# Second sweep of a hybrid encoder layer: key and rotary-query transposes on VectorE in 32x32 blocks, blocks put in place by the loads

## The chip, the cores and the metric

The kernel runs on one core of one Trainium2 chip. The metric is the device time in microseconds of one execution; the shown time of the kernel before is the median of three runs, 1270.41 us (1268.89 to 1271.71). All engines of the core run side by side and wait for each other through semaphores: TensorE (PE in the profile, PEld for its weight loads), VectorE (DVE), ScalarE (ACT), GpSimd (POOL), and SyncE (SP), which here does nothing but issue DMA transfers. A transfer that an engine issues runs on 16 shared DMA engines.

## The reference

One encoder layer over 2048 tokens of width 1024. The input projection feeds two groups of heads, their gated outputs are concatenated and projected, and a residual with layer norm closes the layer. Cut to what the change touches:

```python
h = x @ w_in      # split: g_q g_k g_v g_gate g_lr_f g_lr_b | m_cq m_ckv m_kr m_gate
# group A: gated linear attention, forward and backward scans, 4 heads of 128
o = rms_norm(o_fwd + o_bwd, norm_g)
o_a = o * silu(gate)
# group B: latent attention, 4 heads
q = (rms_norm(c_q, q_norm_g) @ w_uq)            # per head: 128 plain, 64 rotary
kv = (rms_norm(c_kv, kv_norm_g) @ w_ukv)        # per head: 128 key, 128 value
k_r = apply_rope(k_rope, positions)             # one rotary key of 64 for all heads
s = einsum(q_nope, k_nope) + einsum(apply_rope(q_rope), k_r)
o_b = (softmax(s) @ v) * silu(gate)
out = layer_norm(ALPHA * x + concat(o_a, o_b) @ w_out)
```

The kernel takes the key projection into the queries (absorbed weights), so the scores are products of a 128-wide query with the 128-wide normed latent `ckv` itself, and the values are `ckv` too, projected afterwards. Every product is done in three matmuls of a high and a low part (`hi`, `lo`), which is how single precision is kept.

## The kernel before

Tokens are split in 16 chunks of 128. Four parts follow each other.

**Sweep A** goes backward over the chunks and computes most of group A; intermediate tensors go to DRAM.

**Sweep C** (the second sweep, `sweep_c`, about 347 to 583 us) goes forward in eight steps of two chunks. For each chunk it projects `cq`, `ckv` and the rotary key (`c_ip`, PE), norms them, and has PE transpose four 128x128 pieces by a matmul with the identity (`c_tm`, L1368): two of `cq`, one of `ckv`, and one of `krs`, which holds the high and the low part of the rotary key side by side. ACT and DVE then split the results into high and low parts in SBUF (`c_cqTh`, `c_cqTl`, `c_ckvTh`, `c_ckvTl`, `c_krT`). These, `ckvT_h`, `ckvT_l` and `kr`, stay in SBUF for attention, beside the untransposed `vh` and `vl`, which are the high and low parts of `ckv` and serve as values. From `cqT` come the plain queries of a step (`c_pq`) and the rotary queries of a chunk (`c_pqr`); the latter go through the rotation on DVE and POOL (`c_qrf`, `c_qrfa`), two transposes on PE (`c_tq`, L1408), a split (`c_qrTh`, `c_qrTl`), and to DRAM (`c_sqr`, four transfers a step). `c_Ob` to `c_og` finish group A's output of a chunk; `c_oT` transposes it on DVE, which turns every 32x32 block on its own and leaves the blocks where they were, and `c_soT` puts the blocks in place as it stores, in four transfers of 32 partitions whose contiguous pieces are 128 bytes long.

**Attention** runs 16 blocks of one head and 512 queries. `fetch` loads a block's queries: `qh`, `ql`, `rh`, `rl`. The rotary ones have 64 rows, and each is loaded twice, into both halves of the partitions, since `kr` has the high part of the key in one half and the low part in the other. `scores` runs five matmuls per key tile: two with `ckvT_h`, one with `ckvT_l`, two with `kr` (L1562 to L1566).

**The output product** (`OutProj`) loads a chunk's gated outputs of both groups (`load`: `of`, `gr`), multiplies group B's by its gates, splits both in high and low, multiplies with `w_out`, and closes with residual and layer norm.

The order of the work within an engine's queue in sweep C is written by hand: each operation has a place in a table (`PLACE_C`, with other values for the first and the last step), in units of a step, one value for each of the step's two chunks (the tuple) or one for the step. All operations are sorted by step number plus place, and every engine, SP too, runs its own in that order. An instruction that waits holds up whatever stands behind it on its engine. In a step, `tm` of its first chunk stands at 0.532 and of its second at 1.152, which is in the next step's time. The PSUM pool `tr` has two buffers, shared by `tm`, `pqr` and `tq`.

Of the kernel before, what the change touches and what calls it, by code (L numbers as in the profile page):

```python
# [9 lines left out]
F32 = mybir.dt.float32  # L10
F32R = mybir.dt.float32r
# [123 lines left out]
STEP_C = ("gm1", "gm2", "gm3", "gm4", "sgm", "pq", "qah", "qal", "sqa", "sqr")  # L135
CHUNK_C = ("lx", "xh", "xl", "lS", "lq", "lo", "lu", "sqm", "ssm", "rml", "rmd", "cq", "ckv", "krf", "krfa",
    "krsh", "krsl", "vh", "vl", "tm", "cqTh", "cqTl", "ckvTh", "ckvTl", "krT", "pqr", "qrf", "qrfa",
# [3 lines left out]
FETCH_C = ("lx", "xh", "xl")  # L141


PLACE_C = dict(
    ipa=(-0.08, 0.695),
# [6 lines left out]
    tq=(1.06, 1.482),  # L152
# [12 lines left out]
    qrTh=(1.16, 1.587),  # L165
# [11 lines left out]
    qrTl=(1.25, 1.687),  # L177
# [24 lines left out]
    sqr=1.869,  # L202
# [15 lines left out]
PLACE_C_FIRST = dict(  # L218
    ipa=(-1.874, 0.381),
# [6 lines left out]
    tq=(1.11, 1.512),  # L226
# [49 lines left out]
    sqr=1.92,  # L276
# [9 lines left out]
    tq=(0.919, 2.161),  # L286
# [49 lines left out]
    sqr=3.147,  # L336
# [10 lines left out]
class K:  # L347
# [146 lines left out]
    def run(self):  # L494
        tc, nc, ins = self.tc, self.nc, self.ins
        with ExitStack() as top:
# [43 lines left out]
            self.ckvT_h = rp.tile([P, NKT, P], F32R, name="ckvT_h")  # L540
            self.ckvT_l = rp.tile([P, NKT, P], F32R, name="ckvT_l")
            self.kr = rp.tile([P, NKT, P], F32R, name="krs")
# [586 lines left out]

    def split_c(self, xf, j, eng="pool"):  # L1130
        self.hi(self.xch[:, :, j], xf)
        self.lo(self.xcl[:, :, j], xf, self.xch[:, :, j], eng)

    def sweep_c(self):


        with ExitStack() as ctx:
# [17 lines left out]
            for s in steps:  # L1155
                for n in range(8):
                    put("pz", s["st"], self.c_pz, s, n, j=n)
                for n in STEP_C:
                    put(n, s["st"], getattr(self, "c_" + n), s)
            for d in chunks:  # L1160
                for n in range(4):
                    put("ip" + "abcd"[n], d["st"], self.c_ip, d, n, j=d["j"])
                for n in CHUNK_C:
                    if (d["st"] or n not in FETCH_C) and (d["c"] < NCH - 1 or n not in ("Sf1", "Sf2")):
                        put(n, d["st"], getattr(self, "c_" + n), d, j=d["j"])
            for i, place in enumerate((8.23, 9.35)):
# [44 lines left out]
    def scale_w(self, ct):  # L1211
        wa = self.w1.tile([P, H, P], F32, tag=f"qrT{'hl'[ct]}", name=f"wabs{ct}")
# [75 lines left out]
    def c_sqr(self, s):  # L1288
        b, qs = self.of_step(s)
        for t, dst in zip(s["qrT"], self.qr_s[b]):  # L1290
            for pr in range(2):
                self.nc.sync.dma_start(dst[2 * pr:2 * pr + 2, :, qs].rearrange("h d t -> (h d) t"),
# [767 lines left out]
```

## Time and profile before

| | |
|---|---|
| median of the runs shown | 1270.41 us |
| the profiled execution, its own time | 1270.53 us |
| its span (first to last instruction) | 1268.4 us |
| PE busy | 1247.2 us |
| DVE / ACT / POOL busy | 893.5 / 727.9 / 718.6 us |
| DMA engines, share of the span (queue q1) | 43.2% |
| transposes of sweep C on PE: tm, tq | 64, 32 instructions |
| block transposes of oT on DVE | 16, 712 ns each |
| packets under 512 bytes in sweep C (360 to 580 us) | 33629 |

The span is a little shorter than the time of the run, which has 2.1 us around it. In the views of the profile a row names the source line and engine, then what is written and read (`tm<-ident,ckv`). In rows of a timeline the first number is when the instruction starts, the second how long it takes, and brackets hold the idle time of the engine just before it and what ended that. The busy time of PE counts matmuls from their start to a modelled end, and they overlap: one matmul's length is more than the time by which it moves the next. A row of SP is the issue of a transfer; that it has landed is seen in the column "us to landing" of the DMA view or in who waits for it. The chain that ended last follows the work back from the last instruction, each time to what released it.

### The profile page before, as it was taken

How to read it: one execution, taken by the hardware profiler on the slowest of the kernel's cores; microseconds unless marked ns; L12 is line 12 of the kernel's file. 1: busy time of each engine (PE TensorE's matmuls, PEld its weight loads, DVE VectorE, ACT ScalarE, POOL GpSimd, SP SyncE). 2: the span in 40 equal slices, each digit the busy share in tenths (PEclk: the TensorE clock that was granted, in tenths of full speed). 3: DMA queues.
4: the chain of work that ended last, by engine and by line, in shares of the span. 5: the costliest groups of instructions: out<-in, count | busy, mean ns of one | idle time of the engine just before them, and what ended most of it. 6: DMA issues, size and time to landing. Idle time of an engine off the chain costs nothing.

```text
span 1268.4 us, 19649 instructions
## 1 busy us (share of the span) xinstructions
PE 1247.2 (98%) x6950; PEld 1100.2 (87%) x6950; DVE 893.5 (70%) x1610; ACT 727.9 (57%) x1177; POOL 718.6 (57%) x443
## 2 busy tenths in 40 slices
PE   8999999999999999989999999999999999999997
PEld 7999999999899999988788888888888888887886
DVE  6635555553665545564888888888888888389997
ACT  7544343454665444444888888888888888411110
POOL 0132323223265554430798888889999999935541
PEclk9999999999999999999999999999999999999999
DMA  8224555565857766747211111202133120376662
GB/s 297 76 82 124 136 144 137 144 134 159 274 173 211 210 187 204 211 133 199 76 32 53 40 45 42 59 9 59 58 92 92 42 42 26 122 231 195 208 191 100
DMA packets 188546, 160.10 MB, mean 126 GB/s; under 512 B 97206, under 2 KB 139838, under 8 KB 188448
## 3 DMA queue, kind: packets, MB, share of 16 engines
q1 hardware_dynamic: 180384, 156.72, 43.2%
q0 software_dynamic: 672, 2.10, 0.4%
q8 instruction: 55, 0.90, 0.3%
q10 hardware_dynamic: 7392, 0.03, 0.3%
q14 instruction: 43, 0.35, 0.1%
HBM read 102.79 MB, written 56.00 MB: 125 GB/s over the span
## 4 chain that ended last, share of the span: by engine, by line
PE 87%; issue 3%; DMA 3%; POOL 2%; DVE 2%; ACT 2%; SPq 1%; DVEq 0%; POOLq 0%; ACTq 0%
PE pz L1244 7%; PE ipm L1315 5%; PE o L412 5%; PE o L413 5%; PE o L414 4%; PE pS L1562 4%; PE pS L1563 4%; PE pS L1564 4%; PE pS L1565 4%; PE pS L1566 4%; PE ipa L412 4%; PE ipa L414 4%; PE ipa L413 4%; PE ipg L414 2%; PE ipg L413 2%
## 5 line engine op out<-in xcount | busy, mean ns | idle before, releaser
L364 POOL TENSOR_TENSOR pl<-s,ph 128x1024 fp32r<-128x1024 f32 x128 | 306.7, 2415 | 51.5 <-ACT ph L358 48.0
L1584 DVE TENSOR_TENSOR rm<-pS,rm 128x512 f32<-128x512 f32 x210 | 144.8, 690 | 36.3 <-ACT s L1571 30.7
L1571 ACT ACTIVATE s<-pS 128x1024 f32<-128x1024 f32 x128 | 131.2, 1025 | 61.3 <-PE pS L1566 51.7
L1608 DVE TENSOR_TENSOR s<-s,mb 128x1024 f32<-128x1024 f32 x128 | 151.2, 1213 | 8.9 <-PE mb L1602 8.2
L358 ACT ACTIVATE ph<-s 128x1024 fp32r<-128x1024 f32 x128 | 135.0, 1056 | 17.2 <-PE o L414 16.5
L1612 ACT ACTIVATE s<-s 128x1024 f32<-128x1024 f32 x128 | 131.4, 1049 | 9.4 <-DVE s L1608 9.3
L412 PE MATMUL ipa<-wah,xah 128*128 128x384 f32 (+1 forms) x384 | 128.8, 335 | 5.5 <-ACT wah L358 5.5
L413 PE MATMUL ipa<-wal,xah 128*128 128x384 f32 (+1 forms) x384 | 124.5, 324 | 0.0
L414 PE MATMUL ipa<-wah,xal 128*128 128x384 f32 (+1 forms) x384 | 124.5, 324 | 0.0
L1079 POOL TENSOR_TENSOR Sb<-Sb,Us 64x512 f32<-64x512 f32 x15 | 19.9, 1324 | 169.7 <-DVE Us L1071 160.6
L1562 PE MATMUL pS<-qh,ckvT_h 128*128 128x512 f32 x256 | 102.6, 401 | 0.8 <-DVE rm L1584 0.4
L412 PE MATMUL o<-ph,vh 128*128 128x512 f32 x256 | 101.1, 395 | 0.0
L1563 PE MATMUL pS<-ql,ckvT_h 128*128 128x512 f32 x256 | 100.0, 391 | 0.0
L1564 PE MATMUL pS<-qh,ckvT_l 128*128 128x512 f32 x256 | 99.9, 390 | 0.0
L1565 PE MATMUL pS<-rh,krs 128*128 128x512 f32 x256 | 99.9, 390 | 0.0
L1566 PE MATMUL pS<-rl,krs 128*128 128x512 f32 x256 | 99.8, 390 | 0.0
L414 PE MATMUL o<-ph,vl 128*128 128x512 f32 x256 | 99.8, 390 | 0.0
L413 PE MATMUL o<-pl,vh 128*128 128x512 f32 x256 | 99.7, 389 | 0.0
L1635 DVE TENSOR_TENSOR ap<-ap,s 128x512 f32<-128x512 f32 x120 | 83.0, 692 | 2.7 <-ACT s L1612 0.7
L412 PEld LDWEIGHTS ipa<-wah,xah 128*128 128x128 f32 x384 | 73.1, 190 | 8.4 <-ACT wah L358 5.5
L364 POOL TENSOR_TENSOR ol<-of,oh 128x512 fp32r<-128x512 f32 x32 | 43.0, 1344 | 64.3 <-ACT oh L358 64.3
L413 PEld LDWEIGHTS ipa<-wal,xah 128*128 128x128 f32 x384 | 73.2, 191 | 0.8 <-DVE wal L364 0.2
(302 smaller groups left out, 3427.3 us busy)
## 6 DMA issues: line engine op xcount, KB each, us to landing
xcf<-xT_dram SPq DMA_DIRECT2D x16, 512.0 KB, 5.4
xr<-x_dram SPq DMA_DIRECT2D x16, 512.0 KB, 6.3
out_dram<-rr SPq DMA_DIRECT2D x32, 256.0 KB, 2.1
xaf<-xT_dram SPq DMA_DIRECT2D x14, 512.0 KB, 4.2
oib<-oi_s SPq DMA_DIRECT2D x16, 256.0 KB, 3.7
qdb<-qd_s SPq DMA_DIRECT2D x16, 256.0 KB, 3.5
SU<-su_s SPq DMA_DIRECT2D x16, 256.0 KB, 3.9
ub<-u_s SPq DMA_DIRECT2D x16, 256.0 KB, 3.9
```

Of the source, the lines that this page charges most:

```text
L358: return nc.scalar.activation(dst, src, AF.Copy).ins
L364: return e.tensor_tensor(dst, src, hi.bitcast(F32), ALU.subtract).ins
L412: mm(out, ah, bh, start=start, stop=False)
L413: mm(out, ah, bl, start=False, stop=False)
L414: mm(out, al, bh, start=False, stop=stop)
L1562: mm(ps[:, e], kh, qh, start=True, stop=False)
L1563: mm(ps[:, e], kh, ql, start=False, stop=False)
L1564: mm(ps[:, e], kl, qh, start=False, stop=False)
L1565: mm(ps[:, e], kr, rh, start=False, stop=False)
L1566: mm(ps[:, e], kr, rl, start=False, stop=True)
L1584: V.tensor_tensor(d["rm"], src[:, e], d["rm"], ALU.max)
L1608: V.tensor_tensor(s, s, d["mb"][:, None, :].to_broadcast([P, 2, QB]), ALU.subtract)
```

## The change

Four things in sweep C and what reads from it.

**Keys.** For the chunks of the first seven steps `tm` transposes `cq` alone. A new operation `kvx` has DVE turn `vh`, `vl` and `krs` in 32x32 blocks into one tile per step; `skv` stores the tile as it lies, one transfer a step; `kv_load` brings two chunks back, one step and a bit later, in four transfers of 32 partitions, each block at its place. The splits `ckvTh`, `ckvTl` and `krT` go for these chunks: the high and the low part are turned, not split again. The last step's two chunks keep the old way. The three key tensors are now views of one tile, `kvT`.

**Rotary queries.** `tq` is DVE's: one 128x256 block transpose into SBUF. The splits read that tile, both parts go into one tile `qrT` (two buffers), and `sqr` is one transfer a chunk. `fetch` places the blocks: eight transfers a block of attention for `rh` and `rl`, where there were four.

**Gated output of group A.** `soT` stores `oT` as it lies in one transfer; `OutProj.load` places the blocks with four transfers of 32 partitions, where there was one.

**Places.** `tq`, `qrTh`, `qrTl` move back by up to 0.08; in the last step the loads `lq` and `lo`, `soT` and `tq` get other places, `lq` so that the first chunk's comes before the second's. `krs` has two buffers.

```diff
-STEP_C = ("gm1", "gm2", "gm3", "gm4", "sgm", "pq", "qah", "qal", "sqa", "sqr")
+STEP_C = ("gm1", "gm2", "gm3", "gm4", "sgm", "pq", "qah", "qal", "sqa")
...
+LAST_C = ("ckvTh", "ckvTl", "krT")
+KV_LOADS = tuple((2 * s - 4, 2 * s - 2, float(s)) for s in range(2, NCH // 2)) + ((12, 14, 8.27),)
...
 PLACE_C = dict(
+    skv=1.6,
+    kvx=(1.12, 1.44),
...
-    tq=(1.06, 1.482),
+    tq=(1.13, 1.56),
...
-    qrTh=(1.16, 1.587),
+    qrTh=(1.19, 1.62),
...
-    qrTl=(1.25, 1.687),
+    qrTl=(1.26, 1.7),
...
-    sqr=1.869,
+    sqr=(1.4, 1.88),
...
 PLACE_C_LAST = dict(
...
-    tq=(0.919, 2.161),
+    tq=(0.95, 2.1),
...
-    lq=(-0.287, -0.357),
-    lo=(-0.124, 0.045),
+    lq=(-0.357, 0.05),
+    lo=(-0.14, 0.045),
...
-    soT=(1.09, 2.304),
+    soT=(1.29, 2.304),
...
-    sqr=3.147,
+    sqr=(1.6, 3.147),
...
-            self.qr_s = [[dp.tile([H, 64, QB], F32, name=f"r{p}_s{b}") for p in "hl"] for b in range(NQB)]
+            self.qr_s = [dp.tile([2, QB // P, P, 256], F32, name=f"qr_s{b}") for b in range(NQB)]
...
-            self.oa_s = [dp.tile([P, H, P], F32, name=f"oa_s{c}") for c in range(NCH)]
+            self.kv_s = dp.tile([NCH, 3, P, P], F32, name="kv_s")
+            self.oa_s = [dp.tile([H, P, P], F32, name=f"oa_s{c}") for c in range(NCH)]
...
+    def blocks_of(self, src):
+
+        v = src.rearrange("i (b r) m t -> m r (i b) t", b=4)
+        return [(slice(32 * m, 32 * m + 32), v[m]) for m in range(4)]
...
+    def c_kvx(self, d):
+
+        s = d["step"]
+        if "kvx" not in s:
+            s["kvx"] = self.w1.tile([P, 2, 3, P], F32, tag="kvx", name=f"kvx{d['st']}")
+        for i, src in enumerate((self.vh[:, d["c"]], self.vl[:, d["c"]], d["krs"].rearrange("p a d -> p (a d)"))):
+            self.nc.vector.transpose(s["kvx"][:, d["j"], i], src.bitcast(F32))
+
+    def c_skv(self, s):
+        c = 2 * s["st"]
+        self.nc.sync.dma_start(self.kv_s[c:c + 2].rearrange("c i p f -> p (c i) f"),
+                               s["kvx"].rearrange("p a i f -> p (a i) f"))
+
+    def kv_load(self, cs):
+        for r, src in self.blocks_of(self.kv_s[cs].rearrange("c i p (m t) -> (c i) p m t", t=32)):
+            self.nc.sync.dma_start(self.kvT[r, cs].rearrange("p c i (b t) -> p (c i b) t", t=32).bitcast(F32), src)
...
-        for i, src in enumerate((d["cq"][:, 0:P], d["cq"][:, P:2 * P], d["ckv"],
-                                 d["krs"].rearrange("p a d -> p (a d)").bitcast(F32))):
-            self.nc.tensor.transpose(tp[:, i], src, self.ident)
+        src = (d["cq"][:, 0:P], d["cq"][:, P:2 * P])
+        if d["st"] == NCH // 2 - 1:
+            src += d["ckv"], d["krs"].rearrange("p a d -> p (a d)").bitcast(F32)
+        for i, e in enumerate(src):
+            self.nc.tensor.transpose(tp[:, i], e, self.ident)
...
     def c_tq(self, d):
-        tq = d["tq"] = self.tr.tile([P, 4, P], F32, tag="tr", name=f"tq{d['c']}")
-        for pr in range(2):
-            self.nc.tensor.transpose(tq[:, pr], d["qr"][:, 2 * pr:2 * pr + 2].rearrange("p h d -> p (h d)"), self.ident)
+        d["tq"] = self.w1.tile([P, 256], F32, tag="qrx", name=f"qrx{d['c']}")
+        self.nc.vector.transpose(d["tq"], d["qr"].rearrange("p h d -> p (h d)"))
...
     def c_soT(self, d):
-        t = d["oT"].rearrange("p h (a t) -> p h a t", a=4)
-        dst = self.oa_s[d["c"]].rearrange("(a r) h (b t) -> b r h a t", a=4, b=4)
-        for b in range(4):
-            self.nc.sync.dma_start(dst[b], t[32 * b:32 * b + 32])
+        self.nc.sync.dma_start(self.oa_s[d["c"]].rearrange("h p f -> p h f"), d["oT"])
...
-        for p, src in zip("hl", self.qr_s[b]):
+        for n, p in enumerate("hl"):
             q.append(qp.tile([P, QB], F32R, tag="wz", name=f"r{p}{i}"))
-            for r in (slice(0, 64), slice(64, 128)):
-                nc.sync.dma_start(q[-1][r].bitcast(F32), src[h])
+            src = self.qr_s[b][n].rearrange("c (b r) (m t) -> m r (c b) t", b=4, t=32)
+            for r in range(4):
+                nc.sync.dma_start(q[-1][32 * r:32 * r + 32].rearrange("p (c t) -> p c t", t=32).bitcast(F32),
+                                  src[2 * h + r % 2])
...
-        nc.sync.dma_start(of[:, 0], kern.oa_s[c])
+        for r, src in kern.blocks_of(kern.oa_s[c].rearrange("h p (m t) -> h p m t", t=32)):
+            nc.sync.dma_start(of[r, 0].rearrange("p h (b t) -> p (h b) t", t=32), src)
```

More of the change, by code (lines that the diff above doesn't have):

```diff
@@ L218 @@
 PLACE_C_FIRST = dict(
+    skv=1.6,
+    kvx=(1.18, 1.5),
     ipa=(-1.874, 0.381),
@@ L1163, in sweep_c @@
                 for n in CHUNK_C:
+                    late = d["st"] == len(steps) - 1
+                    if n in (LAST_C if not late else ("kvx",)):
+                        continue
                     if (d["st"] or n not in FETCH_C) and (d["c"] < NCH - 1 or n not in ("Sf1", "Sf2")):
                         put(n, d["st"], getattr(self, "c_" + n), d, j=d["j"])
+            for a, b, place in KV_LOADS:
+                todo.append((place, len(todo), self.kv_load, (slice(a, b),)))
             for i, place in enumerate((8.23, 9.35)):
@@ L1351, in c_krsh @@
     def c_krsh(self, d):
-        d["krs"] = self.w1.tile([P, 2, 64], F32R, tag="krs", name=f"krs{d['c']}")
+        d["krs"] = self.w1.tile([P, 2, 64], F32R, tag="krs", name=f"krs{d['c']}", bufs=2)
         self.hi(d["krs"][:, 0], d["kr"][:, 0])
```

33 lines of the change are left out of this document (18 added, 15 removed).

## The prediction

> **What bounds the kernel now.** I read the page first: busy shares, the slices, the chain that ended last. Then, for the second sweep, the windows by step, the waits of PE, the chain of one step in order of time, and the timelines of SP, DVE and PE at the two places where a transfer could come late.
>
> ```profile
> span 1268.4 us, 19649 instructions
> PE 1247.2 (98%) x6950; PEld 1100.2 (87%) x6950; DVE 893.5 (70%) x1610; ACT 727.9 (57%) x1177; POOL 718.6 (57%) x443
> PE 87%; issue 3%; DMA 3%; POOL 2%; DVE 2%; ACT 2%; SPq 1%; DVEq 0%; POOLq 0%; ACTq 0%
> ```
>
> PE is busy 98% of the span and is 87% of the chain. That share alone would not say that a PE instruction taken out shortens anything, so the windows come next (us, then busy time of PE, PEld, DVE, ACT, POOL, then clock, DMA share, GB/s): one middle step of the second sweep, 218 us of that sweep, a stretch of attention, and six chunks of the output product.
>
> ```profile
> 435.36:463.90 28.54, 28.54 (x210) 27.80 (x210) 15.48 (x57) 14.10 (x41) 14.97 (x17) 1.00 0.71 204
> 362.00:580.00 218.00, 214.78 (x1553) 207.90 (x1552) 119.11 (x431) 105.55 (x304) 105.32 (x115) 0.99 0.66 189
> 640.00:1000.00 360.00, 360.00 (x1654) 298.05 (x1653) 312.94 (x419) 301.31 (x324) 317.54 (x136) 1.00 0.20 52
> 1183.74:1249.02 65.28, 65.28 (x290) 54.08 (x289) 63.55 (x89) 8.85 (x23) 31.42 (x24) 1.00 0.57 184
> ```
>
> A middle step lasts 28.54 us and PE has no idle time in it, while DVE works 15.48 and ACT 14.10. So a step is as long as its matmuls take to issue, and the whole sweep lacks only 3.22 us of PE work (218.00 - 214.78). Attention and the output product are as full: what the sweep saves isn't eaten by a later stage that waits for something fixed.
>
> **Transposes removed.** The chain in order of time through 460 to 468 us has what a transpose costs:
>
> ```profile
> 463.68 0.22 PE tq L1408 x2
> 463.90 0.89 PE Ob L1462 x8
> 464.79 0.44 PE tm L1368 x4
> 465.23 2.88 PE pz L1244 x24
> L1368 PE MATMUL tm<-ident,ckv x16: 272/273/273, 363.2 to 576.0; 128*128 128x128 f32 x16
> L1408 PE MATMUL tq<-ident,qrf x32: 270/272/328, 377.9 to 582.7; 128*128 128x128 f32 x32
> ```
>
> Two of tq move the chain by 0.22 us and four of tm by 0.44: 0.11 us each, though the tile views give 272 ns as the length of one. PE is pipelined; the step pays the interval, not the length. The change takes out both tq transposes of 16 chunks (32), and the ckv and krs transposes of 14 chunks, since the last step keeps its own (28). 60 x 0.11 = **6.6 us** off PE. Nothing is added to PE. The Trainium skill (TensorE: Matmul & The Clock Gate, Part 4) gives about 275 ns for a 128x128 transpose inside a kernel; by that 60 would be worth 16.5 us. The trace agrees with it as a length, not as what the next matmul waits.
>
> **VectorE.** Added per chunk: three 128x128 block transposes (kvx) and one 128x256 (tq). Removed: the low part of ckvT. The shapes next to them:
>
> ```profile
> L1014 DVE STREAM_TRANSPOSE ktx<-kd 128x512 f32<-128x512 f32 x10 | 6.7, 674 | 0.0
> ...
> L817 DVE STREAM_TRANSPOSE qx<-ipa 128x256 f32<-128x256 f32 x12 | 5.3, 441 | 0.0
> L1491 DVE STREAM_TRANSPOSE oT<-og 128x512 f32<-128x512 f32 x16 | 11.4, 712 | 0.5
> 467.35 0.42 DVE L364 TENSOR_TENSOR cqT_l<-tm,cqT_h 128x256 fp32r<-128x256 f32 x1
> 469.62 0.28 PE L414 MATMUL pqr<-wqr_h,cqT_l 128*128 128x256 f32 x1
> ```
>
> From 441 and 674 ns, 256 columns cost 0.23 us, so 128 columns take 0.32 and a chunk adds 3 x 0.32 + 0.44 = 1.40 us. By the places in the tables, all four stand in front of cqTl of the step's second chunk, and PE waits for cqTl: it ends at 467.77 and L414, the first matmul that reads cqT_l, issues at 469.62. That is 1.85 us of room, less 0.44 because four transposes ahead of it on PE are gone: 1.41. So the addition just fits and costs **0**; without that cover it is on the path in every step. Upper bound: all four at 0.712, 2.85 us, 1.44 late in 7 steps, 10.1 us. A gain is excluded, since PE has no idle time there to give back. At the first chunk of a step kvx and tq stand where DVE idles before qal. ACT loses two copies a chunk and gains nothing.
>
> **DMA engines and SP.** Key store (skv), key load (kv_load), plain oT store and rotary-query store replace four oT stores a chunk and four rotary stores a step. Packets of 128 bytes exist before as stores only; a window with nothing else in it, then the tail's queue:
>
> ```profile
> DMA packets 544, 0.07 MB, mean 51 GB/s; under 512 B 544, under 2 KB 544, under 8 KB 544
> q1 hardware_dynamic: 544, 0.07, 34.2%
> ...
> q1 hardware_dynamic: 33995, 36.11, 42.8%
> L1497 SPq DMA_DIRECT2D oa_s<-oT x64: 580/632/1392, 375.9 to 587.0; - x64
> L1897 SPq DMA_DIRECT2D of<-oa_s x16: 325/384/791, 940.7 to 1221.1; - x16
> ```
>
> The first window is 1.3 us: 0.342 x 16 x 1.3 us / 544 = 13 ns a packet. The tail (268 us) gives 54 ns for a mean packet of 1062 bytes; on the line between, 512 bytes cost 30 ns. A step's DMA work is 0.71 x 28.54 = 20.3 us. Off: 4096 packets of 13 ns over 16 engines, 3.3. On: 1792 rows of 512 bytes, 3.4, and 3072 loaded pieces of 128 bytes. No load of such pieces can be read here by itself. Bounds 13 ns (same size, stored) and 54 ns (mean load of the tail); I take 13, as the size is the same: 2.5 us, 22.9 of a 27.65 us step. It fits, cost **0**. The step is full at 38 ns. SP loses 8 x 0.63 (oT) and gains about 0.4 x 2 and 4 x 0.63 to 0.95 (kv_load): no more than before. What newly waits on SP is the key store, for kvx of the second chunk; behind it stands the qdb load of the next chunk, whose product comes over half a step later.
>
> **The step before the last.** PE's waits in the sweep, and what led to them:
>
> ```profile
> PE pqr L412 <- DVE rm_t L431: 2.6, 1, 2.6
> ...
> PE pqr L414 <- DVE cqT_l L364: 0.3, 1, 0.3
> PE tq L1408 <- POOL qrf L1403: 0.2, 1, 0.2
> 535.26 9.54 SPq L1423 DMA_DIRECT2D qdb<-qd_s  x2
> 544.89 0.74 SPq L1423 DMA_DIRECT2D SU<-su_s  x1
> 545.72 0.86 SPq L1292 DMA_DIRECT2D rh_s<-qrTh  x2
> 546.67 0.90 SPq L1292 DMA_DIRECT2D rl_s<-qrTl  x2
> 547.62 0.94 SPq L1423 DMA_DIRECT2D oib<-oi_s  x2
> 547.93 1.05 PE L1462 MATMUL Ob<-SU,qdb 128*128 128x128 f32 x8
> 551.40 0.70 DVE L1465 TENSOR_TENSOR Ob<-Ob,oib 128x512 f32<-128x512 f32 x1 [3.51 <-DMA oib<-oi_s]
> ```
>
> That is all of the 3.2 us: SP issues the oib load only at 547.62, behind four rotary stores; DVE stands until 551.40, and cqTl is late. The changed order puts oib of chunk 14 ahead of the last rotary store, about 2.4 us earlier, so DVE could start when Ob is done (548.98). It then has 1.40 us more to do before cqTl, so the stall ends 1.0 earlier, of which 0.44 are transposes already counted: **-0.6**, bounds 0 and -3.2.
>
> **Start of attention.** Loads of the first block's queries, and the matmul that needs the last of them:
>
> ```profile
> 575.03 0.62 SPq L1532 DMA_DIRECT2D qh<-qh_s  x1
> 577.45 1.19 SPq L1536 DMA_DIRECT2D rl<-rl_s  x2
> 583.69 0.39 PE L1566 MATMUL pS<-rl,krs 128*128 128x512 f32 x1
> rl<-rl_s SPq DMA_DIRECT2D x32, 128.0 KB, 4.6
> ```
>
> Issue ends at 578.64 and the data land by about 582.7, 1 us ahead of use. Rotary queries now need eight issues of 0.63 instead of four of 0.6: 2.6 us more. But the oT store that ran just ahead of them (4 x 0.63 us) is now behind, so **0**, bounds 0 and +1.6 (2.6 less the 1 us).
>
> **Output product.** The load of a chunk's gated part is four issues, 2.2 us more SP time ahead of the ob_s load. It is near the path once:
>
> ```profile
> 1115.04 0.53 SPq L1900 DMA_DIRECT2D of<-ob_s  x1
> 1126.02 2.55 POOL L364 TENSOR_TENSOR ol<-of,oh 128x512 fp32r<-128x512 f32 x2 [0.74 <-ACT oh L358]
> 1126.19 0.39 PE L412 MATMUL pmb<-woh,oh 128*128 128x512 f32 x1
> ```
>
> Chunk 4's second low part is done 1.28 us after 1126.02; PE reaches it 13 to 14 matmuls of 0.225 (65.28/290, in the window of six chunks) after 1126.19, 2 us later. 2.2 us more eats that room: **+0.4**, bounds 0 and +1.5.
>
> **Sum.** -6.6 - 0.6 + 0.4 = -6.8 us. The profiled run took 1270.5 (2.1 outside its span), 0.1 above the shown median: 1263.7 for it, **1263.6** for the median. Its own range is -9.8 (whole stall gone) to -3.5 (1.6 and 1.5 paid): 1260.6 to 1266.9.
>
> **Rivals.**
> *VectorE becomes the bound at pqr.* Against it: the two measured shapes. For it: 0.01 us of room. It decides from 1.41 us added; at the 512-column price the steps give 10.1 back: 1270.4 - 6.8 + 10.1 = **1273.7**, slower. Chance 0.10.
> *Short loads are dear.* From 38 ns the step is DMA-bound. At 54 ns it takes 20.4 + 10.4 = 30.8 instead of 27.65, +3.1 in 6 steps; a tail chunk (10.88 us, 0.57 used, 6.2) takes 6.2 + 6.9 = 13.1, +2.2 in some 9: 1263.6 + 18.6 + 19.8 = **1302**. The trace has nothing above 13 ns for that size, but in stores alone. Chance 0.05. The Trainium skill speaks for this one (DMA: Bandwidth & Descriptors, Specifications: under 512 B a transfer falls off line rate by read-modify-write); the 13 ns stores show no such loss, and no run here shows loads.
> *The gain is given back on SP*: a key store or load stands in front of a load and PE waits once a step for an operand. Above 7 us of delay at qdb it shows, 1 us in 6 or 7 steps: **1270**. Against it SP's work does not grow. Chance 0.09.
> *A transpose holds PE for its length*: 60 x 0.272 = 16.3, so **1254**. The 28.54 us step speaks against it. Chance 0.02.
>
> **Numbers.** The forecast has 0.74. A change under 0.2% (2.5 us) can't be told from none. Faster: 0.74 + 0.02 + 0.03 of the SP rival = 0.79; same: 0.05 of SP, 0.03 of VectorE = 0.08; slower 0.13. Range 1259.8 to 1270: the own range, the runs' spread of 1.5 and the SP rival.
>
> **What would show it.** Middle steps of 27.65 us with PE full; 60 fewer transposes; cqT_l ending just ahead of L414, or PE waiting there (VectorE rival); DMA share near 0.82 in a step, and 128-byte loads of 13 ns (or more, DMA rival); the stall before the last step about 2 us; no PE wait for rl or kvT. A middle step at or over 28.5 us would prove the forecast wrong.

## The result, and the profile after

The changed kernel takes **1266.51 us** (median of 8 runs, 1264.55 to 1268.71); the kernel before took 1270.47 us beside it (8 runs). The ratio is 0.9968, with a 95% interval of 0.9959 to 0.9977: 4.0 us faster, with 2.9 to 5.2 inside the interval. The forecast was 1263.6 us with a range of 1259.8 to 1270, so the direction and the range hold, and 2.8 us of the 6.8 forecast did not come.

From the page of the changed kernel, the span, the busy times and the chain that ended last:

```profile
span 1264.5 us, 19632 instructions
PE 1242.3 (98%) x6890; PEld 1094.2 (87%) x6890; DVE 906.0 (72%) x1654; ACT 725.8 (57%) x1149; POOL 721.7 (57%) x443
PE 86%; DVE 5%; DMA 3%; issue 2%; SPq 2%; ACT 1%; POOL 1%; DVEq 0%; POOLq 0%; ACTq 0%
```

PE has 60 instructions fewer (6950 to 6890), exactly the transposes. The bound is still PE, but DVE's share of the chain has gone from 2% to 5%: more of the chain now runs through VectorE. The windows (us, busy time of PE, PEld, DVE, ACT, POOL, clock, DMA share, GB/s) of the same middle step and of 218 us of the second sweep:

```profile
435.46:463.12 27.66, 27.66 (x202) 26.97 (x201) 17.68 (x63) 13.73 (x37) 15.17 (x17) 1.00 0.82 237
362.00:580.00 218.00, 213.51 (x1524) 206.10 (x1523) 134.72 (x479) 106.22 (x281) 107.89 (x117) 0.99 0.75 215
```

A middle step lasts 27.66 us, PE is full in it and the DMA engines are busy 0.82 of it. All three numbers are the forecast's (27.65, full, 0.82). But these 218 us of the sweep now lack 4.49 us of PE work (218.00 - 213.51) where they lacked 3.22 before. Something outside the middle steps became worse. PE's waits in the sweep, in us in total, times, longest:

```profile
PE pqr L418 <- ACT cqT_h L364: 1.4, 1, 1.4
PE pz L1266 <- DVE og L1523: 1.2, 2, 0.9
PE pqr L420 <- DVE cqT_l L370: 1.2, 1, 1.2
...
PE tm L1407 <- ACT cq L1358: 0.5, 1, 0.5
...
PE pq L418 <- DVE og L1523: 0.3, 1, 0.3
```

The two for `cqT_h` and `cqT_l` are the stall before the last step. The others are new. One of 0.28 us for `og`, at 562.67 us, lies in the last step; the rest, 1.6 us, belong to the work of the first two steps. A table shows where the time went. Each entry is the start of one PE instruction in the run's timeline minus the start of the same one in the kernel before, in us; a falling number is time gained. The landmarks are the first `Ob` of the sweep, the transposes `tm` of chunks 4, 12 and 14, the first `mx` of the first and the second block of attention, and the end of the span. Runs other than the first are the experiments below.

| profiled run | sweep starts | chunk 4 | chunk 12 | chunk 14 | attention 1 | attention 2 | end |
|---|---|---|---|---|---|---|---|
| the change | +0.4 | +1.4 | -2.0 | -3.6 | -3.8 | -3.9 | -3.9 |
| x1: rotary store late | +0.2 | +1.3 | -2.2 | -4.3 | -4.5 | -4.5 | -3.3 |
| x2: key store late too | +0.5 | -0.4 | -3.0 | -4.5 | -4.8 | -4.7 | -5.3 |
| x8: chunk 0's transposes late | +0.6 | +1.3 | -2.2 | -2.5 | -3.2 | -3.2 | -2.8 |
| x10: no keys in step 0 | +0.4 | -0.6 | -2.8 | -4.3 | -4.5 | -4.5 | -3.5 |
| x6: old places of lq, lo | +0.6 | +2.2 | -1.1 | -2.3 | -2.5 | -2.5 | -2.5 |
| x12: chunk 12's transposes late | +0.2 | -0.7 | -2.6 | -5.1 | -4.6 | -4.5 | -4.0 |
| x13: and less of the gated part | +0.2 | -0.7 | -1.6 | -4.0 | -3.5 | -3.5 | -5.7 |
| x3: keys alone | +0.4 | +0.6 | +4.0 | +5.2 | +5.2 | +5.3 | +4.3 |
| x4: rotary queries alone | +0.4 | +0.2 | -1.6 | -3.7 | -4.0 | -4.0 | -5.4 |
| x5: gated output alone | 0.0 | 0.0 | 0.0 | -0.8 | -0.8 | -0.8 | -0.1 |
| x9: keys and rotary queries | 0.0 | +1.1 | -0.2 | -1.0 | -1.0 | +2.0 | +0.3 |
| x14: rotary queries and gated output | +0.4 | -0.2 | -2.0 | -3.2 | -3.4 | -3.4 | -2.0 |

The change's row reads: +0.4 before anything changed (two of the runs don't have it, so it belongs to the run); 1.0 lost by chunk 4, where the 14 transposes gone by then should have gained 1.5, so 2.5 behind the forecast; 3.4 gained from chunk 4 to chunk 12 in four steps, 0.86 a step against eight transposes of 0.11; 1.6 more around the stall; then nothing, up to the end. Of the 2.5 us, 1.6 stand in the waits above. Part of the rest is that a wait is counted from the modelled end of the matmul before it, which lies behind the time at which the next one could have started. How far two runs can differ is seen in x6: up to chunk 12 its hand-written order is that of the change, and it stands at +2.2 at chunk 4 where the change has +1.4.

What happens in the first two steps is told by ACT's and SP's timelines there and by the DMA queue from 388 to 400 us. Before:

```profile
q1 hardware_dynamic: 1776, 2.10, 56.4%
```

After:

```profile
398.61 1.03 ACT L1271 ACTIVATE gm<-pz 128x1024 f32<-128x1024 f32 x1 [2.12 <-DMA qr_s<-qrT]
...
q1 hardware_dynamic: 3417, 3.71, 91.3%
```

In the kernel before, the first gate operation `gm1` of step 1 started at 396.29 us, right behind ACT's work on `xch`. Now it stands 2.12 us for a store. Its output tile `gm` has one buffer, which the low part of the plain queries, `ql`, uses as well, so `gm1` must wait until the store of `ql` of step 0 has been read out. (The row puts the wait down to the rotary store, which ends last; with that store moved away, in x8, the row names `ql_s` and the wait is as long.) `gm4` on DVE and `cq` on ACT stand behind the gate operations, `og` behind `gm4`, and PE needs `cq` for `tm` and the PSUM buffer that `og` empties for `pz`.

Why that store is late is seen on SP. Its rows in the change, and below them in x10, an experiment without key transfers in step 0:

```profile
388.96 0.37 SPq L1394 DMA_DIRECT2D kv_s<-kvx  x1
...
389.96 0.83 SPq L1461 DMA_DIRECT2D ub<-u_s  x1
...
391.78 0.52 SPq L1308 DMA_DIRECT2D ql_s<-qal  x1
...
402.25 2.31 SPq L1399 DMA_DIRECT2D kvT<-kv_s  x4
```

```profile
387.18 0.65 SPq L1461 DMA_DIRECT2D ub<-u_s  x1
...
391.69 0.52 SPq L1308 DMA_DIRECT2D ql_s<-qal  x1
```

In the change SP stands from 386.87 us at the key store, until DVE has done `kvx` of chunk 1 (388.93). Behind it stand the loads `qdb` and `ub`, which are then issued at 389.38 and 389.96, right ahead of the query stores; in x10 they go out at 386.67 and 387.18, in the kernel before at 383.99 and 384.47. The store of `ql` itself is issued at nearly the same time in all three (391.78, 391.69, 391.24), with more transfers just ahead of it in the change. The first key load is issued only at 402.25, when `gm1` has long begun, so it has no part in this wait.

### The profile page after: what moved, and what is told of

Same layout as the page of the kernel before. It is cut to its first block, busy times and chain, and to the rows that moved or that the text cites. A ratio compares the mean times of both kernels' runs of the same rounds, so it can differ in the third digit from the quotient of the medians.

```text
span 1264.5 us, 19632 instructions
## 1 busy us (share of the span) xinstructions
PE 1242.3 (98%) x6890; PEld 1094.2 (87%) x6890; DVE 906.0 (72%) x1654; ACT 725.8 (57%) x1149; POOL 721.7 (57%) x443
## 4 chain that ended last, share of the span: by engine, by line
PE 86%; DVE 5%; DMA 3%; issue 2%; SPq 2%; ACT 1%; POOL 1%; DVEq 0%; POOLq 0%; ACTq 0%
PE pz L1266 7%; PE ipm L1335 5%; PE o L418 5%; PE o L419 5%; PE o L420 5%; PE pS L1599 4%; PE pS L1600 4%; PE pS L1602 4%; PE pS L1601 4%; PE pS L1603 4%; PE ipa L418 4%; PE ipa L420 4%; PE ipa L419 4%; PE ipg L420 2%; PE ipg L418 2%; PE ipg L419 2%
## 5 line engine op out<-in xcount | busy, mean ns | idle before, releaser
L1599 PE MATMUL pS<-qh,kvT 128*128 128x512 f32 x256 | 102.4, 400 | 0.8 <-DVE rm L1621 0.4
L1600 PE MATMUL pS<-ql,kvT 128*128 128x512 f32 x256 | 99.9, 390 | 0.0
L1602 PE MATMUL pS<-rh,kvT 128*128 128x512 f32 x256 | 99.9, 390 | 0.0
L1601 PE MATMUL pS<-qh,kvT 128*128 128x512 f32 x256 | 99.8, 390 | 0.0
L1603 PE MATMUL pS<-rl,kvT 128*128 128x512 f32 x256 | 99.7, 390 | 0.0
```

Of the source, the lines that this page charges most:

```text
L1599: mm(ps[:, e], kh, qh, start=True, stop=False)
L1600: mm(ps[:, e], kh, ql, start=False, stop=False)
L1601: mm(ps[:, e], kl, qh, start=False, stop=False)
L1602: mm(ps[:, e], kr, rh, start=False, stop=False)
L1603: mm(ps[:, e], kr, rl, start=False, stop=True)
```

## The experiments

The kernel before took 1270.67, 1270.31, 1270.18 and 1270.00 us in the four groups of runs below (x1, x3, x4, x6; x2, x8, x9, x10; x5, x12, x14; x13). Every ratio is to the kernel before of the same group.

**x1, rotary store of the first step late.** The change moves the store of chunk 0's rotary queries from the end of the step to 1.42, where SP waits for it. x1 moves it back, in the table of the first step:

```diff
-    sqr=(1.42, 1.92),
+    sqr=(1.915, 1.92),
```

> Changed kernel, but in the first step the store of the first chunk's rotary queries stands at 1.915 instead of 1.42 in the order. Theory S (SP waits): in the changed kernel SP stands 7 us behind this store, the loads behind it and the query stores then run in one bunch, the store of the low queries lands late, and ACT waits 2.1 us for its tile before it can gate step 1; PE loses 1.4 us at 408 to 410 us for it. Then that wait of ACT falls under 0.5 us, the two PE waits at 408 and 409 us go, and the time is 1.4 to 1.8 us under the changed kernel: about 1264.9. Rival V (VectorE): 0.9 us of block transposes in front of the group A output are what PE waits for; then the waits stay and the time is 1266.5.

Measured: 1267.68 us, ratio 0.9981 [0.9973, 0.9990]. PE's two waits at 408 and 409 us stayed at 0.52 and 0.88 us, and chunk 4 stood at +1.3. The theory of the early rotary store falls: SP still stood at the key store, until 388.80, and `gm1` 2.14 us for `ql_s`.

**x3, x4, x6: the parts by themselves, and the old places.** x3 is the kernel before with the key part (`kvx`, `c_skv`, `kv_load`, two instead of four transposes in `c_tm`); x4 is the kernel before with the rotary part (`c_tq`, `c_qrTh`, `c_qrTl`, `c_sqr`, the query loads, and their new places); x6 is the change with the old places of two loads in the last step:

```diff
-    lq=(-0.357, 0.05),
-    lo=(-0.14, 0.045),
+    lq=(-0.287, -0.357),
+    lo=(-0.124, 0.045),
```

> Kernel before with the key part alone (kvx, its store and load, 28 transposes fewer), all other places as before. 28 x 0.11 = 3.1 us off PE. S: without the early rotary store SP is free, nothing is lost in the first steps, but 0.6 us of kvx stand in front of cqTl in the stall before the last step: 1270.5 - 3.1 + 0.6 = 1268.0. V: the 0.6 us also show at the start of the sweep, another 0.6 to 0.8 lost: 1268.7.

> Kernel before with the rotary-query part alone (block transpose on VectorE, two stores a step, eight loads a block of attention, 32 transposes fewer) and its places of the changed kernel. 32 x 0.11 = 3.5 us off. S: the store of chunk 0's rotary queries stands early in SP's queue here too, so the wait of ACT for the query tile and the PE waits near 409 us are there: 1.4 to 1.8 lost, 1268.6. V: 0.4 us of VectorE alone is too little to show: 1267.0.

> Changed kernel with the old places of lq and lo in the last step. If the new order of these loads is what shortened the stall before the last step, as in the prediction's sum (oib of chunk 14 about 2.4 us earlier), PE's waits there grow from 2.5 us to 4 or 5 and the time to about 1268.5. Rival: the stall is set by VectorE's work alone, the order does nothing: 1266.5.

Measured: x3 1273.94 us, ratio 1.0023 [1.0013, 1.0033]; x4 1266.40, 0.9969 [0.9956, 0.9981]; x6 1267.88, 0.9979 [0.9970, 0.9988]. The rotary part alone brings as much as the whole change, and the key part alone makes the kernel slower. PE's waits in the sweep of x3 say how:

```profile
PE tq L1445 <- POOL qrf L1440: 4.8, 5, 1.9
PE pqr L418 <- ACT Ob L432: 3.5, 1, 3.5
```

By these waits, DVE with the key transposes gets later to the rotation of the rotary queries, POOL's last addition `qrf` behind it is late, and PE, which in x3 still has `tq` to do, stands in five steps, up to 1.9 us. (The second row is the old stall before the last step.) 28 transposes (3.1 us) were taken off PE and 4.8 us of waiting came in their place. This is read from the trace; no run moves the key transposes in x3. In the whole change `tq` is DVE's, so nothing on PE waits for `qrf` so soon. In x4 the loss before chunk 4 is small (+0.2 there, where the change has +1.4). In x6 the stall before the last step is the same as in the change (1.35 and 1.15 us), so the new places of `lq` and `lo` do nothing for it; x6 loses in the first two steps, which they don't touch. It does not test the forecast's reason for the shorter stall, that `oib` of chunk 14 goes ahead of the last rotary store: in x6 it does so too (issued at 543.97 us, the store at 544.48), since that store's own place went from 1.869 to 1.88.

**x2, x8, x10: which part of step 0 costs the first two steps?** x2 moves the key store and the first key load as well as the rotary store; x8 moves DVE's transposes of chunk 0 behind `og`; x10 leaves the keys of the first step on PE (and starts `KV_LOADS` a step later):

```diff
# x2
-    skv=1.6,
+    skv=1.95,
-    sqr=(1.42, 1.92),
+    sqr=(1.915, 1.92),
-KV_LOADS = tuple((2 * s - 4, 2 * s - 2, float(s)) for s in range(2, NCH // 2)) + ((12, 14, 8.27),)
+KV_LOADS = tuple((2 * s - 4, 2 * s - 2, s + 0.55 * (s == 2)) for s in range(2, NCH // 2)) + ((12, 14, 8.27),)
# x8
-    kvx=(1.18, 1.5),
+    kvx=(1.4, 1.5),
-    tq=(1.18, 1.53),
+    tq=(1.4005, 1.53),
-    qrTh=(1.276, 1.598),
+    qrTh=(1.403, 1.598),
-    qrTl=(1.322, 1.703),
+    qrTl=(1.406, 1.703),
-    sqr=(1.42, 1.92),
+    sqr=(1.915, 1.92),
# x10
-                    late = d["st"] == len(steps) - 1
+                    late = d["st"] in (0, len(steps) - 1)
-                if s["st"] < len(steps) - 1:
+                if 0 < s["st"] < len(steps) - 1:
                     put("skv", s["st"], self.c_skv, s)
-        if d["st"] == NCH // 2 - 1:
+        if d["st"] in (0, NCH // 2 - 1):
             src += d["ckv"], d["krs"].rearrange("p a d -> p (a d)").bitcast(F32)
```

> The changed kernel with three places of the first step moved back: key store at 1.95 instead of 1.6, first key load at 2.55 instead of 2.0, first rotary store at 1.915. Theory Q (the key store and load of the first step fill the DMA engines just when the unrotated queries are stored, so gm1 of step 1, which reuses their buffer, starts late and og behind it): gm1 waits at most 0.9 us instead of 2.12, PE's waits for og fall from 1.5 us to 0.3, time 1265.0 us. Theory V (VectorE's transposes of chunk 0 stand ahead of og): gm1 may come earlier, PE still waits 1.5 us for og; 1266.5 us. Bounds from the run with the rotary store alone moved: 1267.7 us if nothing changes.

> The changed kernel with VectorE's transposes of chunk 0 (keys and rotary queries) and the split of the latter placed behind og of chunk 2, at 1.40 to 1.406 instead of 1.18 to 1.32; the first rotary store at 1.915. Theory V (they stand ahead of og, which PE waits for in steps 0 and 1): PE's waits for og fall from 1.5 us to 0.3 or less, time 1265.2 us. Theory Q (it is the late store of the unrotated queries, through gm1): gm1 still waits about 2 us, PE still 1.2 us for og; 1266.5 us or a little above.

> The changed kernel, but the two chunks of the first step have their keys turned on PE and split on ACT and VectorE as before the change; no key store and load for them. Theory: the loss of 2.7 us in the first two steps belongs to the key part in the first step; then the loss falls to the 0.7 us that the rotary part alone showed, less 0.44 us for four transposes that return to PE: 1266.5 - 2.0 + 0.4 = 1264.9 us. Rival: the loss comes with the rotary part and the gated part as well, and the key part of the first step adds nothing: 1266.5 + 0.4 = 1266.9 us.

Measured: x2 1266.41 us, ratio 0.9968 [0.9957, 0.9979]; x8 1267.26, 0.9975 [0.9965, 0.9985]; x10 1266.59, 0.9969 [0.9957, 0.9981]. ACT's row of `gm1` in x8, then in x2, and x2's DMA queue from 388 to 400 us:

```profile
398.50 1.03 ACT L1271 ACTIVATE gm<-pz 128x1024 f32<-128x1024 f32 x1 [2.28 <-DMA ql_s<-qal]
```

```profile
396.50 1.01 ACT L1271 ACTIVATE gm<-pz 128x1024 f32<-128x1024 f32 x1
...
q1 hardware_dynamic: 2128, 2.29, 65.1%
```

PE's waits of x2 from 345 to 560 us, without those before the last step:

```profile
...
PE pz L1266 <- DVE og L1523: 0.3, 1, 0.3
PE pq L418 <- DVE og L1523: 0.3, 1, 0.3
```

In x2 the DMA engines are busy 65.1% instead of 91.3%, `gm1` waits for nothing, the 0.9 us wait for `og` is gone, and chunk 4 stands at -0.4 instead of +1.4. x10, without the keys of step 0, does the same (`gm1` at 396.31, chunk 4 at -0.6, four transposes dearer). x8 moved the VectorE work and kept the transfers: `gm1` still waits 2.28 us and chunk 4 stays at +1.3. So the loss in the first two steps comes with the key store of step 0, as it stands in the order, and goes through `gm1` and the shared buffer. This is shown. That the link between the two is the loads held behind the store is read from SP's rows, and x4 agrees: it has no key store, but there SP stands at the early rotary store until 384.10 us and issues a store of `oT` in four behind it, so that `qdb` and `ub` go out at 389.27 and 389.74, and `gm1` waits 0.88 us. The busy share of the DMA engines does not tell the cases apart: in the same window x10 has 81.1% and no wait, x1 79.7% and 2.14 us.

As a speed-up of the whole it is not shown: the medians of x2 and x10 agree with the change's within their intervals of about 1.4 us to either side, although x2's profiled span is 1.4 us shorter than the change's. The profiled run of x2 took 1264.91 us, 1.5 us less than its own median, and where its other runs lose this is not known. x4 and x13 were profiled 1.6 and 1.2 us below their medians, so the ends of the rows in the table are not medians either.

**x9, x5, x14: the gated output part.** x9 is the change with four stores and one load for `oa_s` again; x5 is the kernel before with the plain store and the four loads; x14 is x4 with them:

```diff
-        self.nc.sync.dma_start(self.oa_s[d["c"]].rearrange("h p f -> p h f"), d["oT"])
+        for b in range(4):
+            self.nc.sync.dma_start(dst[b], t[32 * b:32 * b + 32])
-        for r, src in kern.blocks_of(kern.oa_s[c].rearrange("h p (m t) -> h p m t", t=32)):
-            nc.sync.dma_start(of[r, 0].rearrange("p h (b t) -> p (h b) t", t=32), src)
+        nc.sync.dma_start(of[:, 0], kern.oa_s[c])
```

> The changed kernel without the gated-output part (oT stored by four issues into its turned layout and loaded by one, as before the change). Prediction's step: the four-issue load costs 0.4 us at chunk 4 and nothing else, the old store nothing: 1266.1 us. Rival: the gated part is what the tail of the changed kernel lacks against the run with the rotary part alone (there the tail gained 1.4 us over the point where attention begins): 1265.1 us. Second rival: the four store issues per chunk, back on SP among the key store and load, delay the loads of the sweep: above 1266.9 us, with new PE waits in the middle steps.

> The kernel before with the gated-output part alone: oT stored as it lies by one issue, loaded by four. Prediction's step: it costs 0.4 us at chunk 4 of the output product, and the three store issues it saves on SP are worth nothing: 1270.8 us. Theory SP (with the key and rotary parts in, it saved 7 us, since SP at the end of the sweep is then overfull): without them SP has room, so it is worth nothing here either, 1270.4 to 1270.8 us. Rival: it brings the oib load of chunk 15 and the stores behind it earlier by 1.9 us each chunk and so shortens a stall by itself: 1268 us.

> The kernel before with the rotary and the gated-output parts, keys left on PE as before. Against the rotary part alone (1266.4 us). Theory SP: the gated part is only worth something where the key loads fill SP at the end of the sweep; here it costs its 0.4 us at chunk 4: 1266.8 us; and the key part is then worth at most 0.3 us in the whole change. Rival (the gated part shortens SP's way through each step and with it the waits of steps 0 and 1 and at the start of attention): under 1265.5 us.

Measured: x9 1273.59 us, ratio 1.0022 [1.0013, 1.0031]; x5 1272.03, 1.0014 [1.0006, 1.0023]; x14 1268.15, 0.9983 [0.9974, 0.9992]. So by the medians the gated part, which was costed at +0.4, costs about 2 us by itself or beside the rotary part, and is worth 7 us in the whole change; between the profiled spans of x9 and the change it is 4.2 us. In x9 PE waits twice for `og` in the middle steps, 0.5 us at 465 us and 0.9 at 494, as its second rival had it: from chunk 4 to chunk 12 x9 gains 1.4 us, the change 3.4. The large loss is 3 us in the first block of attention (-1.0 to +2.0 in the table). SP's, DVE's and ACT's timelines there in x9:

```profile
595.10 0.57 SPq L1308 DMA_DIRECT2D qh_s<-qah  x1
600.53 0.56 SPq L1308 DMA_DIRECT2D ql_s<-qal  x1
601.19 0.78 SPq L1834 DMA_DIRECT2D wvf<-wv_dram  x1
...
599.28 1.22 DVE L370 TENSOR_TENSOR qal<-pq,qah 128x1024 fp32r<-128x1024 f32 x1
...
604.96 0.73 ACT L1766 ACTIVATE wvf<-wvf,gkv_c 128x512 f32<-128x512 f32 x1 [4.05 <-DMA wvf<-wv_dram]
```

In the change itself:

```profile
591.88 0.51 SPq L1308 DMA_DIRECT2D ql_s<-qal  x1
592.49 0.57 SPq L1831 DMA_DIRECT2D wvf<-wv_dram  x1
...
598.23 0.72 ACT L1763 ACTIVATE wvf<-wvf,gkv_c 128x512 f32<-128x512 f32 x1
```

The eight issues for a block's rotary queries, the key load and eight stores of the last gated outputs fill SP up to 595.67 us in x9. It then stands 4.9 us for one store, that of the last step's `ql`. DVE makes `ql` (`qal`) only at 599.28, behind twelve of attention's maxima; in the change it does so at 590.63, behind seven. A load that stands behind this store, that of the value weights `wvf`, is issued at 601.19 instead of 592.49 us, ACT waits 4.05 us for it with the copies of the scores behind, then DVE's maxima, then PE (0.9 and 2.3 us). Of all traces x9 alone has `qal` behind more than seven maxima, and x9 alone has this wait. The store of the gates ahead of `qal`, which must have been read out of the shared buffer first, is issued at 584.19 in x9 and at 580.12 in the change, so the one-issue store of `oT` does make room on SP; why `qal` stands so much later in DVE's queue no run shows. x9 is also the kernel whose runs differ most: seven of its twelve had a granted clock of 0.993 to 0.995 where the others had 0.997, and those at 0.997 took 1270.6 to 1272.1 us, with a median of 1271.84, so 1.8 of the 7 us go with the lower clock. Not all is accounted for: the profiled runs of x5 and x9 were the shortest of their kernels (1270.11 of 1270.11 to 1273.92, and 1270.56 of 1270.56 to 1275.92), and the trace of x5 ends 0.1 us ahead of the kernel before, so it does not hold the 1.9 us that its median lost.

What the part costs in the traces is in the output product, where PE's waits in the change and in x9 are

```profile
PE pmb L420 <- POOL ol L370: 0.7, 1, 0.7
PE rt L1726 <- ACT rt L1732: 0.7, 1, 0.7
```

```profile
PE rt L1729 <- ACT rt L1735: 0.4, 1, 0.4
```

The wait for `ol`, which comes at chunk 6, is in each of the nine traces that load chunk 6's gated outputs in four issues, with 0.5 to 1.1 us, and in none of the five others. From the second block of attention to the end x9 gains 1.7 us and x4 1.5, whereas the change gains nothing and x14 loses 1.4. The change and its variants x1, x2, x6, x8, x10 and x12, whose output product is the same, lie between a loss of 1.2 and a gain of 0.6 us, so a single row says little.

**x12 and x13: the stall before the last step, and less of the gated part.** x12 is x2 with the block transposes and the split of chunk 12 moved behind `cqT_l` of chunk 13. x13 is x12 with the gated outputs of chunks 0 to 4 and 6 stored and loaded as before:

```diff
# x12
+PLACE_C_C12 = dict(kvx=(1.285,), tq=(1.286,), qrTh=(1.287,), qrTl=(1.288,))
+                p = (st == len(steps) - 2 and j == 0 and PLACE_C_C12.get(n)) or p
# x13
+TURNED = (0, 1, 2, 3, 4, 6)
-        self.nc.sync.dma_start(self.oa_s[d["c"]].rearrange("h p f -> p h f"), d["oT"])
+        if d["c"] in TURNED:
...
```

> The changed kernel with the three places of the first step moved back (as in the earlier run of that), and the block transposes and the split of chunk 12 (kvx, tq, qrTh, qrTl) moved behind cqTl of chunk 13, from 7.12 to 7.26 on to 7.285 to 7.288. Theory W (what is left of the stall before the last step is VectorE's own new work: 0.93 us of transposes ahead of the rotary product that frees ACT for cqT_h, then 0.52 us of the low split ahead of cqT_l): PE's two waits there fall from 1.36 and 1.15 us to about 0.4 and 0.6, the span from 1263.1 to 1261.7 us, median 1265.0 us. Rival (ACT and VectorE are late there for the chain og, oT, root mean square, whatever lies between; or the moved work makes the gated output of chunk 14 late): the two waits stay within 0.3 us in sum, or a new wait of PE for og comes behind; 1266.4 us.

> The run with chunk 12's transposes moved, and in it the gated output of chunks 0 to 4 and 6 stored and loaded as before the change (four issues to store, one to load), that of the others as in the change. Theory T (the four-issue loads cost the output product some 1.3 us, above all at chunk 6, while the one-issue stores pay on SP at the end of the sweep): PE's wait for ol at chunk 6 is gone (0.72 us in the changed kernel), the start of attention stays without a wait, span about 1263.4 us, median 1265.0 us. Rival (the stores pay as much in the early steps: with four issues there SP is late for qdb and oib, and og late behind): new PE waits for og in steps 1 to 4 of 0.3 to 0.9 us each take it all back, 1266.0 us or more.

DVE's, ACT's and PE's rows of the changed kernel before the last step show what stands in the way there:

```profile
546.81 0.70 DVE L1503 TENSOR_TENSOR Ob<-Ob,oib 128x512 f32<-128x512 f32 x1 [0.28 <-PE Ob L1500]
...
550.09 0.30 DVE L1390 STREAM_TRANSPOSE kvx<-vh 128x128 f32<-128x128 f32 x1
...
550.70 0.40 DVE L1446 STREAM_TRANSPOSE qrx<-qrf 128x256 f32<-128x256 f32 x1
...
551.50 0.17 ACT L432 ACTIVATE ipm<-rm_l 128x2 f32<-128x2 f32 x1 [1.09 <-DVE rope L1544]
551.61 0.37 ACT L364 ACTIVATE cqT_h<-tm 128x256 fp32r<-128x256 f32 x1
...
552.03 0.38 PE L418 MATMUL pqr<-wqr_h,cqT_h 128*128 128x256 f32 x1 [1.36 <-ACT cqT_h L364]
```

The 3.51 us for the `oib` load is gone. From 550.09 to 551.02 DVE does the four new transposes, ACT waits for the rotation behind them, and `cqT_h` waits in ACT's queue. PE's waits of x12 from 345 to 600 us:

```profile
PE pz L1268 <- DVE og L1525: 1.8, 2, 0.9
PE pq L419 <- DVE og L1525: 0.8, 2, 0.5
PE pqr L421 <- DVE cqT_l L371: 0.7, 1, 0.7
PE ipm L1337 <- POOL xcl L371: 0.6, 1, 0.6
PE pqr L419 <- ACT cqT_h L365: 0.4, 1, 0.4
```

Measured: x12 1265.98 us, ratio 0.9967 [0.9955, 0.9979]; x13 1265.85, 0.9966 [0.9954, 0.9978]. In x12 the two waits fall from 1.4 and 1.2 us to 0.4 and 0.7, as expected of DVE's transposes; then 0.6, 0.5 and 0.9 us for `xcl` and `og` come behind, and nearly all is given back: from chunk 12 to attention x12 gains 2.0 us, x2 1.7. Theory and rival are both right, one after the other. In x13 no wait of 0.3 us or more is left in the output product, and from the second block of attention to the end it gains 2.2 us where x12 loses 0.5; but with the four-issue stores back in the early steps it has lost 1.1 by chunk 12 against x12, with new waits of 0.6 us for `cq` and 0.2 for `og`. Both are equal to the change within their intervals. No version beat it clearly.

## Why the forecast held, and where it failed

**Transposes, -6.6: right.** The chain of a middle step of the change has `tm` at 0.22 us for two, as before for `tq`, and no `tq`:

```profile
449.61 0.22 PE tm L1407 x2
```

A step is 0.88 us shorter, eight times 0.11, and the middle steps keep that to within 0.1 us. The rival by which a transpose holds PE for its length falls, and with it the 275 ns of the Trainium skill (TensorE: Matmul & The Clock Gate, Part 4) as a price: the trace has 273 ns as the length and 0.11 us as what a step pays.

**VectorE, 0: right in the middle steps, with a wrong working, and failed in its cover.** Groups of DVE by shape in the change (us in total, mean ns of one):

```profile
L1446 DVE STREAM_TRANSPOSE qrx<-qrf 128x256 f32<-128x256 f32 x16 | 6.8, 424 | 6.2 <-POOL qrf L1442 6.2
...
L1390 DVE STREAM_TRANSPOSE kvx<-vl 128x128 f32<-128x128 f32 x14 | 3.8, 269 | 0.0
```

The four transposes take 0.93 us in a row (550.09 to 551.02, when the next instruction starts) and not 1.40: 128 columns are 0.27 us long and not 0.32, and each starts before the one ahead has ended. That gives room: in a middle step `cqT_l` ends 0.63 us ahead of its matmul, not 0.01:

```profile
440.80 0.41 DVE L370 TENSOR_TENSOR cqT_l<-tm,cqT_h 128x256 fp32r<-128x256 f32 x1
...
441.84 0.28 PE L420 MATMUL pqr<-wqr_h,cqT_l 128*128 128x256 f32 x1
```

But the cover was looked for at one consumer, `pqr`. In x3 the same DVE work is late for another, `tq` behind POOL, and costs 4.8 us. In the change this consumer had been taken off PE by the rotary part, which the forecast did not see: it priced the parts one by one and added them. They don't add: the medians give +3.3 for the keys, -4.3 for the rotary queries and +1.9 for the gated output alone, +0.9 in sum, and -4.0 together. (The new places of the last step's `lq`, `lo` and `soT` are in none of the three.)

**DMA engines and SP, 0: this is the step that failed.** The share in a middle step came out at 0.82 as forecast, and the rival of dear short loads falls. A stretch of attention from 662 to 667 us with nothing but 128-byte pieces being loaded:

```profile
DMA packets 3447, 0.43 MB, mean 85 GB/s; under 512 B 3447, under 2 KB 3447, under 8 KB 3447
## 3 DMA queue, kind: packets, MB, share of 16 engines
q1 hardware_dynamic: 3447, 0.43, 77.5%
```

0.775 x 16 x 5 us / 3447 is 18 ns a packet, above the 13 taken and far under the 38 from which a step would be full. The prediction set against the rule that speaks of a loss under 512 bytes (the Trainium skill, DMA: Bandwidth & Descriptors, Specifications) that the 13 ns stores show no such loss. By rate that was a misreading: 128 bytes in 13 ns of one engine are 9.8 bytes a ns, and in 18 ns 7.1, where the tail's mean packet of 1062 bytes in 54 ns had 19.7. So the trace agrees with the rule on the rate, and the prediction was right only on what it costs here: 3072 pieces of 18 ns over 16 engines are 3.5 us a step, and they fit.

What failed is a wait on SP that the prediction named and put at nothing. "What newly waits on SP is the key store", it said, with the `qdb` load behind it, and it asked only whether that load comes too late for its own product. It does not. But once released, in step 0, the loads go out right ahead of the query stores, the store of `ql` lands late, and the buffer that it holds makes `gm1` 2.12 us late. Against the 1.5 us that the first two steps should have gained, 1.0 was lost; x2 and x10 bring most of it back in the trace. The rival of a gain given back on SP had the right queue, 0.09 of the chance, and the wrong place: not an operand late once a step, but a buffer late once in the sweep.

**The stall, -0.6: right.** It went from 3.2 to 2.5 us (1.36 and 1.15). The load of `oib` comes before it is needed and DVE goes on when `Ob` is done, as the step said: it is issued at 542.67 us, ahead of the rotary store at 543.20. What is late next is DVE's own new work, as it said too, and x12 shows that by taking it away. The new places of `lq` and `lo` are not what did it (x6); the rotary store's place and its fewer issues remain, and no run parts these two.

**Start of attention, 0: right, and by the cover named.** The change has no wait there that the kernel before had not (table: -3.8, -3.9). The eight issues were costed at 0 since the `oT` store that ran just ahead of them moves behind, and so it did: the last issue for the first block ends at 575.63 us, with the store at 577.94, where before it ended at 578.64. What the prediction did not look at is the rest of SP's row up to the end of the sweep. With the four-issue stores back, x9 loses 3 us there, twice the bound of 1.6, at `wvf` behind the store of `ql` and not at `rl`.

**Output product, +0.4: the net came out near by luck, the place was wrong.** Chunk 4 costs nothing. PE's timelines of the change and of before show a product of column sums, 0.36 us long in the chain, that stands right ahead of chunk 4 in the one and right ahead of chunk 6 in the other:

```profile
1122.34 0.60 PE L1708 MATMUL sx<-ident,acc 128*128 128x128 f32 x4
```

```profile
1147.95 0.60 PE L1671 MATMUL sx<-ident,acc 128*128 128x128 f32 x4
```

The wait for `ol` is 0.7 us, at chunk 6, and the waits for `rt`, 1.4 us before, are 0.7 now, so that the change comes out even. That is luck: x3, x4 and x9, which lack the part, have only 0.4 to 0.9 us of waits for `rt`. Against the same kernel without the part (x9 from the second block on, -1.7 us) it costs more than its bound of 1.5.

## What to carry to other kernels

When work moves from one engine to another, list every consumer of the engine that receives it, and price the parts together: one part may take away the consumer that another makes late. When a new store has to wait in a queue ordered by hand, ask not only whether the loads behind it come too late for their own use, but also which transfers they will run into when they are let go, and which buffers those hold; a mean DMA share of the step does not show it. What stands last in the row pays for a wait ahead of it, however little it has to do with the change.

## What had not been expected of the hardware

The low split of the rotary queries has the same shape as before, but both its inputs now lie in SBUF, where one lay in PSUM. DVE's rows of that tile (min, median, max ns), the change and before:

```profile
L370 DVE TENSOR_TENSOR qrT<-qrx,qrT x16: 402/595/1100, 383.7 to 580.9; 128x256 fp32r<-128x256 f32 x16
```

```profile
L364 DVE TENSOR_TENSOR qrTl<-tq,qrTh x16: 406/414/425, 382.7 to 584.1; 128x256 fp32r<-128x256 f32 x16
```

It varies from 402 to 1100 ns, where it took 406 to 425. In the trace of the change the ten that took 517 ns or more each ran beside instructions of POOL for 0.47 us or longer, the 1100 ns one for 0.82, and the six that took 402 to 425 had at most 0.18 us of POOL beside them. Before, with one input in PSUM, one that ran beside POOL for its whole length took 414 ns. So POOL's work beside it goes with the slow ones; no run was made to test it. And a 128x128 block transpose is 267 to 302 ns long but moves the next by 0.19 to 0.23 us in a row of three.
